# Two more pairs of hidden tiles with seven products, unscaled token blocks, and weight sums made in DRAM

## The chip, the cores and the metric

One Trainium2 core runs the whole kernel. The metric is device time in microseconds (us) of one execution; the profile adds one execution seen from inside.

## The reference

One decoder layer on 512 tokens of width 1024, in float32:

```python
x = x + 0.5 * rms_norm(swiglu(rms_norm(x, g1), w1_in, w1_out), g1_post)      # first half
h = rms_norm(x, g2); q, k, v, u = split(h @ w_mix_in)
x = x + rms_norm(concat(attention(q, k, v), s5(u)) @ w_mix_out, g2_post)     # mixing
x = x + 0.5 * rms_norm(swiglu(rms_norm(x, g3), w2_in, w2_out), g3_post)      # second half
# swiglu(h) = (silu(h @ gate) * (h @ up)) @ w_out, gate and up 1024 x 2816
# rms_norm(x, g) = x * rsqrt(mean(x*x) + 1e-6) * g
```

The change is in the second half, with preparations for it in the first half and in the boundary ahead of the second half.

## The kernel before

**Arithmetic.** Each float32 operand `t` of a product is split into a high part (`hi`, a cast on ACT) and the rest (`lo = t - hi`, a subtraction on DVE or POOL); a product is three matmuls, high x high, high x low, low x high (`mm3`). The helper `wsplit` splits weights, `split` splits activations.

**Hidden tiles.** The hidden width 2816 is 22 tiles of 128. A *plain* tile `f` takes two weight blocks (gate and up, 128 x 1024 each) against all 512 tokens: 24 matmuls a block. From tile `NSTD` on, tiles go in *pairs* with a seven-product scheme: gate and up, each halved along the 1024 inputs, are the four weight blocks a11, a12, a21, a22 (each 512 inputs for two tiles), and the tokens are halved too. A pair has seven products of 24 matmuls over 256 tokens in place of eight: in order a11, a12, c2, c1, c3, c2 + a12 and a22, with the sums c3 = a11 + a21, c2 = c3 + a22 and c1 = a21 + a22 made on DVE by `pair`. The token side of the products is four blocks as they are or subtracted (b11, b21, b22, n1) and three more sums (n2, t3, t4, in tiles `tq`). `pair` reuses the banks `wx`, `wy` and `wq` and ends with Silu, the multiplication with up, and the split into `ah`, `al`.

**Before the change** `NSTD = (8, 6)`: the first half has eight plain tiles and seven pairs, the second half six plain tiles and eight pairs. Tiles 0 and 1 of the second half are computed in `boundary`, tiles 2 to 5 in `swiglu_half` (`products`, matmuls `gu`). While they run, the token blocks are scaled by the norm's gain and by its per-token factor r (`seven`/`sums`, line 533), summed and split. The transposes of x to token-major rows for the end (`tokens_first`, matmuls `xt`) are put between these matmuls by hooks, and so are the two steps of the norm's sums (`late[0]`, `late[1]`: a matmul `st`, a small operation `nv` on DVE, a power on POOL, a matmul `rp`).

**Boundary.** `boundary` ends one part and begins the next: it adds the last output products (`yt`), and for each half of the tokens and each of eight rows of blocks `prep` forms the new x and its split on DVE and ACT, and `begin` issues 12 matmuls of the next part (`first`). POOL adds up squares.

**Output.** The hidden tiles are multiplied with the output weights in three rounds of six tiles (`outp`, matmuls `yo`) and a last one of four (`finish`, matmuls `yt`), which normalises and stores rows.

**Order.** Instructions wrapped in `fix` keep their program order on their engine; the others are placed by a scheduler that goes by program order as priority. Loads are issued from SP into `wraw` (three buffers), `wa` and `wx`; the split weights go to a ring of four (`whi`, `wlo`). DVE, ACT and POOL run ahead of PE as far as these rings allow. POOL does not issue any transfer.

Of the kernel before, what the change touches and what calls it, by code (L numbers as in the profile page):

```python
# [29 lines left out]
NSTD = (8, 6)  # L30
# [14 lines left out]
class Layer:  # L45
# [30 lines left out]


# [195 lines left out]
    def boundary(self, y, tail, ipost, half, inext, chunks):  # L273
# [40 lines left out]
        def prep(h, k, fix=lambda i: i):  # L314
# [5 lines left out]
            self.split(xh(k)[:, hs[h]], xl(k)[:, hs[h]], xk, self.g(inext, k), fix)  # L320
            self.sq_acc(acc2[:, hs[h]], xk, k == 0, nc.gpsimd)
# [46 lines left out]
        for k in range(KD):  # L368
            if k > 1:
                prep(0, k, fx if k > 5 else lambda i: i)  # L370
            begin(0, k)
            if k == 2:
                post[1][0](late, fix=fx)
            if k == 4:
                rr[1] = post[1][1]()
        for k in range(KD):
            prep(1, k)
            begin(1, k)
            if k == 3:
                pre[0][0](fixp=fx)  # L380
            if k == 6:
                pre[0][1]()
        self.xh, self.xl = xh, xl
# [6 lines left out]
    def ffn(self, n, first, scope):  # L390
# [42 lines left out]
        def outp(i, ms=range(KD), tails=None, hold=0):  # L433
# [3 lines left out]
            def part(m, k0, k1):  # L437
# [15 lines left out]
                else:  # L453
                    nc.vector.tensor_tensor(out=y(m), in0=b[m], in1=y(m), op=ALU.add)
# [20 lines left out]
        prep = sums(True)  # L475
# [5 lines left out]
        for m in range(2, KD):  # L481
# [3 lines left out]
            outp(0, (m,))  # L485
        for f in range(NSTD[0], NF, 2):
            pair(f, f in (NSTD[0], 14))
# [23 lines left out]
    def seven(self, fin, w_in, ig, r, ah, al):  # L511
# [13 lines left out]
        def sums(early=False):  # L525
# [13 lines left out]
            more[0] = (yield) or fin  # L539
            if early:  # L540
                self.pad(more[0], 192)
# [4 lines left out]
            bh, bl = [self.b16(n, F32R) for n in ("bh", "bl")] if early else (None, None)  # L546
            v = lambda t, i: t.rearrange("p (q k) c -> p q (k c)", q=4)[:, i]

            def plain(*ts):
                for t in ts:  # L550
                    i = len(blocks)
                    blocks.append((v(bh, i), v(bl, i)))
                    self.split(*blocks[i], t)

            if early:
                plain(b11)
            V.scalar_tensor_tensor(out=n2, in0=n1, scalar=-1.0, in1=b22, op0=ALU.mult, op1=ALU.subtract)
            if early:
                plain(b21)
# [6 lines left out]
            if early:  # L566
                plain(b22, n1)
# [4 lines left out]
            if not early:  # L572
                yield
                bh, bl = [self.b16(n, F32R) for n in ("bh", "bl")]
                plain(b11, b21, b22, n1)
            yield

        def block(f, up, kh):
            if up:
                t = wx() if kh else more[0].tile([P, 1024], F32, name="wa", tag="wa")  # L580
# [3 lines left out]
            nc.sync.dma_start(out=t.rearrange("p (f c) -> p f c", f=2), in_=src)  # L584
            return t
# [922 lines left out]
```

## Time and profile before

| | |
|---|---|
| median of 3 runs | 916.98 us (916.5 to 918.2) |
| the profiled execution | 916.19 us, span 914.2 us |
| busy in the span | PE 898.9, DVE 656.0, ACT 442.0, POOL 217.5 us |
| first half, mixing, second half begin at about | 0, 386, 585 us |
| plain tiles 2 to 5 of the second half | 584.72 to 634.36 us |
| moved by transfers | 106.81 MB, 117 GB/s mean |

A row of a stage gives its length, then busy time and number of instructions by engine; PE is TensorE's matmuls, PEld its weight loads, which overlap them. A row of a group gives line, engine, operation, out<-in, shapes and count, then busy time and mean duration (ns), then idle time before it and what ended that.

### The profile page before, as it was taken

To read this page: it belongs to the slowest core of one execution; us is meant where nothing else is said; L and a number is where in the kernel's file an instruction comes from. 1 tells how busy PE (TensorE), PEld (TensorE's weight loads), DVE (VectorE), ACT (ScalarE), POOL (GpSimd) and SP (SyncE) were. 2 spreads that over 40 slices of the span, in tenths; PEclk is the share of its full clock that TensorE was granted. 3 is DMA by queue.
4 is the path that set the end of the run, shared out by engine and by line. 5 is a ranking of instruction groups with operands and counts; after the bars stand their busy time and mean duration, and the time that the engine had idled before them with its cause. 6 is when DMAs were issued, how large, how long until landed. Compare 5 with 4: busy or idle time off the path is not lost.

```text
span 914.2 us, 15367 instructions
## 1 busy us (share of the span) xinstructions
PE 898.9 (98%) x6169; PEld 801.4 (88%) x6169; DVE 656.0 (72%) x1071; ACT 442.0 (48%) x685; POOL 217.5 (24%) x127
## 2 busy tenths in 40 slices
PE   9999999999999999999999999999999999999996
PEld 7787789998999989978777889888899989998995
DVE  6999786755678666758898567898368557855756
ACT  6263763553355543525745654573355514541542
POOL 0423301322123134500000025523222222221321
PEclk9999999999999999999999999999999999999999
DMA  8223662334231262283321452145222422332222
GB/s 277 94 70 115 196 248 76 107 102 137 77 119 61 68 194 86 92 221 109 116 70 51 153 167 71 29 179 180 97 93 99 133 92 93 116 116 92 92 93 92
DMA packets 47734, 106.81 MB, mean 117 GB/s; under 512 B 7824, under 2 KB 11152, under 8 KB 47120
## 3 DMA queue, kind: packets, MB, share of 16 engines
q1 hardware_dynamic: 46080, 102.21, 34.5%
q10 hardware_dynamic: 1584, 3.63, 1.1%
q8 instruction: 48, 0.79, 0.3%
q14 instruction: 22, 0.18, 0.1%
HBM read 96.13 MB, written 9.70 MB: 116 GB/s over the span
## 4 chain that ended last, share of the span: by engine, by line
PE 79%; DVE 6%; issue 2%; DMA 2%; ACT 1%; POOLq 0%; POOL 0%; DVEq 0%; SPq 0%; ACTq 0%
PE yo L144 21%; PE wx L144 18%; PE wq L144 9%; PE yt L144 6%; PE wy L144 4%; PE gu L144 4%; PE prj L144 4%; PE first L144 3%; PE prv L144 2%; PE mo L144 2%; PE ys L144 1%; PE st L144 1%; DMA w1d<-w1s 1%; PE pt L1098 1%; PE sc L144 1%
## 5 line engine op out<-in xcount | busy, mean ns | idle before, releaser
L117 ACT CAST whi<-wraw 128x1024 fp32r<-128x1024 f32 (+5 forms) x128 | 124.0, 976 | 160.3 <-PE yo L144 65.5
L119 POOL TENSOR_TENSOR wlo<-wraw,whi 128x1024 fp32r<-128x1024 f32 (+1 forms) x41 | 109.2, 2666 | 297.6 <-ACT whi L117 290.3
L119 DVE TENSOR_TENSOR wlo<-wraw,whi 128x1024 fp32r<-128x1024 f32 (+5 forms) x87 | 107.4, 1242 | 75.7 <-ACT whi L117 75.6
L144 PE MATMUL wx<-tq,whi 128*128 128x256 f32 x720 | 124.7, 276 | 0.0
L144 PEld LDWEIGHTS wx<-tq,whi 128*128 128x128 f32 x720 | 108.3, 188 | 0.0
L119 DVE TENSOR_TENSOR wlo<-wsum,whi 128x1024 fp32r<-128x1024 f32 x60 | 73.6, 1227 | 46.5 <-ACT whi L117 46.4
L117 ACT CAST whi<-wsum 128x1024 fp32r<-128x1024 f32 x60 | 63.0, 1050 | 81.8 <-PE yo L144 28.1
L144 PE MATMUL wx<-tq,wlo 128*128 128x256 f32 x360 | 99.4, 276 | 0.0
L119 POOL TENSOR_TENSOR wlo<-wx,whi 128x1024 fp32r<-128x1024 f32 x15 | 41.5, 2764 | 176.3 <-ACT whi L117 128.5
L144 PEld LDWEIGHTS wx<-tq,wlo 128*128 128x128 f32 x360 | 67.6, 188 | 0.0
L144 PE MATMUL gu<-xh,whi 128*128 128x512 f32 x168 | 67.2, 400 | 0.0
L144 PE MATMUL gu<-xh,wlo 128*128 128x512 f32 x168 | 65.7, 391 | 1.1 <-POOL wlo L119 1.1
L144 PE MATMUL wq<-bh,whi 128*128 128x256 f32 x240 | 66.2, 276 | 0.0
L144 PE MATMUL wq<-bl,whi 128*128 128x256 f32 x240 | 66.2, 276 | 0.0
L144 PE MATMUL wq<-bh,wlo 128*128 128x256 f32 x240 | 66.2, 276 | 0.0
L144 PE MATMUL gu<-xl,whi 128*128 128x512 f32 x168 | 65.5, 390 | 0.0
L144 PE MATMUL yo<-ah,whi 128*128 128x512 f32 x144 | 56.3, 391 | 0.0
L144 PE MATMUL yo<-al,whi 128*128 128x512 f32 x144 | 56.1, 389 | 0.0
L144 PE MATMUL yo<-wlo,ah 128*128 128x512 f32 x144 | 56.0, 389 | 0.0
L144 PE MATMUL yo<-whi,ah 128*128 128x512 f32 x144 | 56.0, 389 | 0.0
L144 PE MATMUL yo<-ah,wlo 128*128 128x512 f32 x144 | 56.0, 389 | 0.0
L144 PE MATMUL yo<-whi,al 128*128 128x512 f32 x144 | 56.0, 389 | 0.0
(267 smaller groups left out, 2385.0 us busy)
## 6 DMA issues: line engine op xcount, KB each, us to landing
wraw<-w1i SPq DMA_DIRECT2D x28, 512.0 KB, 3.7
wraw<-w2i SPq DMA_DIRECT2D x28, 512.0 KB, 3.6
wraw<-w2o SPq DMA_DIRECT2D x18, 512.0 KB, 3.7
wraw<-wmi SPq DMA_DIRECT2D x12, 512.0 KB, 4.1
wraw<-w1o SPq DMA_DIRECT2D x8, 512.0 KB, 4.2
wa<-w2i SPq DMA_DIRECT2D x8, 512.0 KB, 3.7
wx<-w2i SPq DMA_DIRECT2D x8, 512.0 KB, 4.0
wa<-w1i SPq DMA_DIRECT2D x7, 512.0 KB, 3.6
```

Source lines behind the costliest of these rows:

```text
L117: fix(self.nc.scalar.copy(out=hi, in_=raw))
L119: fix(eng.tensor_tensor(out=lo, in0=raw, in1=hi.bitcast(F32), op=ALU.subtract))
L144: i = self.nc.tensor.matmul(*a, **k)
L1098: self.fix(nc.tensor.transpose(b[i][:, o:o + P], sc[:, c:c + P], self.ident))
```

## The change

1. `NSTD = (8, 2)`: in the second half tiles 2 to 5 become pairs 2 and 4, ten pairs in all.
2. The pairs of the second half take token blocks that are not scaled by r: three of the four plain blocks are views of `xh`, `xl` themselves. The gate sum is multiplied by r in `pair` (DVE), up is not; r comes back per row in `finish` as `r4`. In `hidden` one multiplication goes.
3. The boundary keeps an unrounded copy of the gained x (`wide`, ACT, one per `prep`) and makes two token sums from it in eight steps (`wide_sums`, DVE). The others are made between the products of pair 2 (`begun`, `further`, `last`).
4. For every pair c3 and c1, and for the pairs 2 and 4 also c2 and c2 + a12, are made in DRAM: a copy issued from SP and an accumulating transfer issued from POOL, 512 KB each. They are spread over the first half and its boundary: each call of `more` counts one, and each 1.6 counts issue one transfer. `pair` then loads the sums (`whole`).
5. The first two weight blocks of pair 2 are loaded and split in the boundary (`self.first`), into a tile of their own.
6. Hooks between the products of pairs 2 and 4 take over the transposes and the norm's steps.

```diff
-NSTD = (8, 6)
+NSTD = (8, 2)
+EARLY = (2, 4)
+PACE = 1.6
...
+    def block_sums(self):
...
+        copy = lambda o, i: self.dma(out=o, in_=i)
+        plus = lambda o, i: self.fix(nc.gpsimd.dma_start(out=o, in_=i, accum_op=ALU.add))
+        t = lambda f, c: self.csum[f, c]
+        stages = (lambda f: copy(t(f, 3), src(f, 0, 0)), lambda f: copy(t(f, 1), src(f, 1, 0)),
+                  lambda f: plus(t(f, 3), src(f, 1, 0)), lambda f: plus(t(f, 1), src(f, 1, 1)),
+                  lambda f: copy(t(f, 2), t(f, 3)), lambda f: plus(t(f, 2), src(f, 1, 1)),
+                  lambda f: copy(t(f, 4), t(f, 2)), lambda f: plus(t(f, 4), src(f, 0, 1)))
+        for n in range(len(fs) + 1):
+            todo = []
+            if n:
+                todo += [(2, fs[n - 1]), (3, fs[n - 1])]
+            if n < len(fs):
+                todo += [(0, fs[n]), (1, fs[n])]
+            if n > 2:
+                todo.append((4 + (n - 3) // 2, EARLY[(n - 3) % 2]))
...
@@ boundary
             self.split(xh(k)[:, hs[h]], xl(k)[:, hs[h]], xk, self.g(inext, k), fix)
+            if wide:
+                fix(nc.scalar.activation(out=t, in_=xk, func=AF.Copy, scale=self.g(inext, k)))
...
             begin(0, k)
+            self.more()
...
+        if wide:
+            wide = wide(y)
         for k in range(KD):
             prep(1, k)
             begin(1, k)
+            if wide and k:
+                wide(k - 1)
...
@@ ffn
                 products(f)
+                self.more(2 + (f > 2))
...
@@ pair
-            a21, a22 = block(f, 1, 0), block(f, 1, 1)
-            c3 = wsum()
-            add(a11, a21, c3)
-            c2 = wsum()
-            add(c3, a22, c2)
-            times(X, cut(c2), n2, False)
+            then(1)
+            if four:
+                c2 = whole(f, 2)
+            else:
+                if made:
+                    c3, a22 = whole(f, 3), block(f, 1, 1)
+                else:
...
+            times(X, cut(c2), tq[0], False, 2 in lead)
...
+            if made:
+                V.tensor_tensor(out=gt, in0=gt, in1=r.unsqueeze(1).to_broadcast([P, 2, S]), op=ALU.mult)
             nc.scalar.activation(out=gt, in_=gt, func=AF.Silu)
...
+    def wide_sums(self, gx):
...
+        for kh in range(2):
+            raw = self.wp.tile([P, 1024], F32, name="wraw", tag="wraw", bufs=3)
+            self.nc.sync.dma_start(out=raw.rearrange("p (f c) -> p f c", f=2), in_=src(kh))
+            hi, lo = (room[:, kh, i] for i in range(2))
+            self.wsplit(raw, hi, lo)
...
+            if k < 4:
+                V.tensor_tensor(out=h(k, 0), in0=h(k, 0), in1=h(k, 1), op=ALU.subtract)
+            else:
+                V.scalar_tensor_tensor(out=self.n2[:, (k - 4) * HT:(k - 3) * HT], in0=h(k - 4, 0), scalar=-1.0, in1=h(k, 1),
+                                       op0=ALU.mult, op1=ALU.subtract)
...
@@ swiglu_half
+        each = {i: step for i in range(6)}
+        pair(2, (2,), hooks={**each, 0: begun, 1: further, 2: late[1], 3: last}, ahead=self.first)
+        hidden(0)
+        hidden(1)
...
+        pair(4, hooks=each)
+        step(9)
...
-        for f in range(NSTD[1], NF, 2):
-            pair(f, f in (NSTD[1], 12, 18), f == NF - 2)
+        for f in range(6, NF, 2):
+            pair(f, (0,) if f in (6, 12, 18) else (), f == NF - 2)
...
@@ finish
-            fx(V.tensor_tensor(out=yg[b, i], in0=at(y, b, i), in1=self.gt[d][:, sl], op=ALU.mult))
+            fx(V.scalar_tensor_tensor(out=yg[b, i], in0=at(y, b, i), scalar=r4[:, b:b + 1], in1=self.gt[d][:, sl],
+                                      op0=ALU.mult, op1=ALU.mult))
```

In the first half `more` is called by `ffn` after its plain tiles and output products and by `pair` between its products.

More of the change, by code (lines that the diff above doesn't have):

```diff
@@ L565, in sums @@
             yield
-            if early:
-                plain(b22, n1)
+            plain(b22, n1)
             yield
@@ L571, in sums, with pairs @@
             self.split(*tq[2], t4)
[L572 to L575, printed above, removed]
             yield
+        room = lambda: more[0].tile([P, 1024], F32, name="wa", tag="wa")
+        return sums, self.pairs(w_in, blocks, tq, wsum, gp, (room, wx), r, ah, al)
+    def pairs(self, w_in, blocks, tq, wsum, gp, rooms, r, ah, al, csum=None):
+        nc, V = self.nc, self.nc.vector
+        wa, wx = rooms
         def block(f, up, kh):
-            if up:
-                t = wx() if kh else more[0].tile([P, 1024], F32, name="wa", tag="wa")
+            if up and (kh or not csum):
+                t = wx() if kh else wa()
             else:
@@ L605, in keep, with pair @@
             return t
-        def pair(f, lead=False, late=False):
-            (b11, b21, b22, n1), (n2, t3, t4) = blocks, tq
+        def pair(f, lead=(), late=False, hooks={}, ahead=None):
             add = lambda x, z, t: V.tensor_tensor(out=t, in0=x, in1=z, op=ALU.add)
@@ L611, in pair @@
             half = lambda t, h: t[:, :, h * HT:(h + 1) * HT]
+            then = lambda i: hooks[i]() if i in hooks else None if csum else self.more()
+            made = bool(csum)
+            four = made and (f, 2) in csum
             gt = p2(gp())
             X = self.bank("wx")
-            a11 = block(f, 0, 0)
-            times(X, cut(a11), b11, True, lead)
+            if not ahead:
+                a11 = block(f, 0, 0)
+                h11 = cut(a11)
+            else:
+                h11, h12 = ahead
@@ L616, in pair @@
+            times(X, h11, blocks[0], True, 0 in lead)
             s1 = keep(X)
-            a12 = block(f, 0, 1)
-            h12 = cut(a12, True)
+            if not ahead:
+                a12 = block(f, 0, 1)
+                h12 = cut(a12, True)
+            then(0)
             Y = self.bank("wy")
-            times(Y, h12, b21, True)
+            times(Y, h12, blocks[1], True)
             V.tensor_tensor(out=half(gt, 0), in0=p2(Y), in1=p2(s1), op=ALU.add)
-            a21, a22 = block(f, 1, 0), block(f, 1, 1)
@@ L639, in pair @@
             nc.scalar.activation(out=gt, in_=gt, func=AF.Silu)
-            times(X, cut(a22, True), t4, False)
+            then(5)
+            times(X, cut(a22, not ahead), tq[2], False)
             s = f % RING
@@ L699, in outp, with begun, further, last @@
                         V.tensor_tensor(out=y(b, d), in0=b4[b], in1=y(b, d), op=ALU.add)
[L701 to L716 removed]
+        tq[0] = put(0, n2)
+        pair = self.pairs(w_in, blocks, tq, lambda: fin.tile([P, 1024], F32, name="wsum", tag="wsum", bufs=3),
+                          lambda: fin.tile([P, 1024], F32, name="gp", tag="gp"), (None, lambda: fin.tile([P, 1024], F32, name="wx", tag="wx", bufs=2)), r, ah, al, self.csum)
+        def begun():
+            blocks[3] = put(3, part(gx, 0, 0))
+            step()
+        def further():
+            third()
+            late[0]()
+        def last():
+            fourth()
+            step()
+        each = {i: step for i in range(6)}
+        pair(2, (2,), hooks={**each, 0: begun, 1: further, 2: late[1], 3: last}, ahead=self.first)
+        hidden(0)
+        hidden(1)
         self.gt = [self.acct() for _ in range(2)]
@@ L1430, in run, with more @@
         first = self.start(chunks, ipre)
+        back = self.block_sums()
+        owed = [0]
+        def more(n=1):
+            owed[0] += n
+            while owed[0] >= PACE:
+                owed[0] -= PACE
+                next(back, None)
+        self.more = more
         for p, q in zip(parts, parts[1:] + " "):
```

150 lines of the change are left out of this document (92 added, 58 removed).

## The prediction

> **What bounds the kernel now.** I read the page first (busy times, queues, chain), then the busy time by stage around the second half, then what TensorE waited for, then single stretches of DVE, ACT and POOL where the change puts work.
>
> ```profile
> span 914.2 us, 15367 instructions
> PE 898.9 (98%) x6169; PEld 801.4 (88%) x6169; DVE 656.0 (72%) x1071; ACT 442.0 (48%) x685; POOL 217.5 (24%) x127
> q1 hardware_dynamic: 46080, 102.21, 34.5%
> PE 79%; DVE 6%; issue 2%; DMA 2%; ACT 1%; POOLq 0%; POOL 0%; DVEq 0%; SPq 0%; ACTq 0%
> ```
>
> TensorE is busy for 898.9 of 914.2 us and carries 79% of the chain; all its idle time is 15.3 us. A change can win much only by taking matmuls away, and can lose wherever it makes one wait. The second half by stage (us, then busy time and count of PE, PEld, DVE, ACT, POOL, the clock, the DMA share, GB/s):
>
> ```profile
> 584.72:634.36 49.64, 48.44 (x234) 40.00 (x233) 46.22 (x54) 27.84 (x38) 19.01 (x7) 1.00 0.46 159
> 607.16:612.60 5.44, 5.44 (x25) 4.50 (x24) 5.44 (x9) 5.44 (x10) 0.00 (x0) 1.00 0.13 50
> 667.00:686.19 19.19, 19.19 (x170) 19.18 (x169) 11.93 (x12) 10.36 (x13) 4.79 (x2) 1.00 0.33 108
> 686.19:705.23 19.04, 19.04 (x170) 19.04 (x169) 15.44 (x16) 10.72 (x12) 5.92 (x2) 1.00 0.31 111
> ...
> PE xt L505 <- DVE nv L205: 1.2, 1, 1.2
> ...
> L117 ACT CAST whi<-wraw 128x1024 fp32r<-128x1024 f32 x7 | 7.4, 1053 | 8.7 <-PE wq L144 5.2 <-PE wx L144 3.6
> ```
>
> The first row is the stage that the change rewrites: tiles 2 to 5 with plain matmuls, the transposes of x between them. The second is one plain 128x1024 weight block against 512 tokens (24 matmuls): 5.44 us. The third and fourth are the first two pairs, seven products each: 19.04 us, that is 2.72 for a product, and 0.15 more where the lead splits one matmul in two. The fifth is the only wait of PE in that stage that the trace names, 1.2 us. The last, from the first three pairs, is the cast that splits a loaded block: 1.05 us, and the idle time before it ends when PE frees room (`wq`, `wx`), not when a load lands.
>
> **The change part by part.**
>
> *Products.* Tiles 2 to 5 are 8 plain blocks, 8 x 5.44 = 43.52 us. Two pairs are 14 products, 14 x 2.72 = 38.08 us. Gain 5.44, less 0.15 for the lead split that pair 2 gets in addition. The eight groups of transposes and the sums of the norm (49.64 - 43.52 - 1.2 = 4.9 us) keep their number and only move, so they cost the same. The wait of 1.2 hangs on the old order (the sums' result stands in DVE's queue behind the scaling of x); that queue goes, so I take it out and price the new waits on their own. Most that can be won: 5.44 - 0.15 + 1.20 = 6.49 us.
>
> *Work removed from DVE.* Sixteen scalings, sums and splits of the x blocks leave this stage; two weight sums per pair go from pair 6 on (1.22 us each, below), and one 1.22 us product with r per pair comes. PE does not wait in the pair stage now, and the cover (DVE 15.44 of 19.04 us) gets better, so this is worth nothing.
>
> *The boundary before the second half.* ACT gets 16 scaled copies of x, DVE eight subtractions of 128x256, and two weight blocks are split there where one was.
>
> ```profile
> 551.26:584.72 33.46, 32.92 (x280) 32.24 (x280) 27.74 (x57) 16.84 (x39) 16.96 (x20) 1.00 0.15 49
> L319 DVE TENSOR_TENSOR x<-ymix,x 128x256 f32<-128x256 f32 x16 | 10.0, 639 | 0.1
> L317 DVE SCALAR_TENSOR_TENSOR ymix<-ymix,sm,rp 128x256 f32<-128x256 f32 x16 | 7.2, 470 | 0.0
> L302 DVE TENSOR_TENSOR ymix<-yt,ymix 128x256 f32<-128x256 f32 x2 | 0.8, 414 | 0.0
> L119 DVE TENSOR_TENSOR tq<-wraw,tq 128x1024 fp32r<-128x1024 f32 x1 | 1.2, 1212 | 0.0
> L176 ACT ACTIVATE sq<-x 128x256 f32<-128x256 f32 x14 | 5.6, 403 | 0.8 <-POOL acc L178 0.8
> 580.84 0.48 DVE L167 SCALAR_TENSOR_TENSOR xl<-x,sm,xh 128x256 fp32r<-128x256 f32 x1 [0.58 <-ACT xh L166]
> 583.27 0.37 PE L144 MATMUL first<-xh,whi 128*128 128x256 f32 x1
> ```
>
> DVE is busy 27.74 of 33.46 us here. Seven of the eight steps stand ahead of the last block: 4 x 0.41 + 3 x 0.47 = 3.05 us, and the second weight split adds 1.21: 4.26 us. DVE's last result is ready at 580.84 + 0.48 = 581.32 and PE takes it at 583.27, 1.95 us later; DVE also idled 0.58 us before it. So 4.26 - 1.95 - 0.58 = 1.7 us reach PE. ACT's 16 copies at the 0.40 of a square (6.4 us) and one more cast (1.05) fit its 33.46 - 16.84 = 16.6 us of idle time. Bounds: 0, if the scheduler finds other gaps (DVE has 5.7 us of them), to 4.3 with no slack used. I take 1.7.
>
> *Pairs 2 and 4.* Pair 2 starts on the token blocks as they are and on weights already split, so its first two products (5.44 us) wait for nothing. By the end of those the split of n2 and of the loaded sum c2 must be done, two times a cast of 1.05 and a subtraction of 1.21 on two engines in turn: some 3.5 us, inside 5.44. Later products need one such split per 2.72 us, besides the third and fourth token sums (1.22 each, and their splits). In 19 us DVE has about 10 operations of 1.2 and three of 0.69, 14 us: it fits, with little air, and the norm's sums now have only one product (2.72 us) between their two PE steps. Bounds 0 (all inside) to 2.5 (twice the old wait); I take 0.6, half the old one, since DVE's queue here is shorter than before.
>
> *The sums in DRAM.* Ten pairs times two copies and two accumulating transfers, and two of each more for the two early pairs: 24 copies on SP's queue and 24 accumulates on POOL's, 512 KB each, one for every 1.6 calls, all issued before the attention part begins. All loads together hold 16 engines for 34.5% of 914.2 = 315 us for 102.21 MB, so 512 KB cost 1.62 us of all engines. By stage, before:
>
> ```profile
> 60.00:145.00 85.00, 83.03 (x436) 67.48 (x435) 68.54 (x99) 47.94 (x80) 20.84 (x9) 1.00 0.52 170
> 145.00:340.00 195.00, 195.00 (x1458) 184.70 (x1457) 129.34 (x131) 92.80 (x107) 47.96 (x20) 1.00 0.32 103
> ...
> PE gu L144 <- POOL wlo L119: 1.1, 1, 1.1
> 178.78 3.51 POOL L119 TENSOR_TENSOR wlo<-wx,whi 128x1024 fp32r<-128x1024 f32 x1 [11.26 <-ACT whi L117]
> 185.66 0.39 PE L144 MATMUL wx<-tq,whi 128*128 128x256 f32 x2
> 368.00 0.71 POOL L207 TENSOR_TENSOR p<-nv,mhalf 128x2 f32<-128x2 f32 x1 [2.37 <-DVE nv L205]
> 170.84 0.34 SPq L123 DMA_DIRECT2D wraw<-w1o  x1
> wraw<-w2i SPq DMA_DIRECT2D x28, 512.0 KB, 3.6
> ```
>
> Some 14 steps fall into the first stage: 14 x 1.62 = 23 us, a share of 0.52 + 0.27 = 0.79; 30 into the second, 0.32 + 0.25 = 0.57. If an accumulate cost double, 0.90 and 0.70. Both stay under 1, and in the pairs the casts wait for PE and not for loads, so bandwidth costs little. POOL is the open point: no row of this kernel shows a transfer issued from POOL. An accumulate also waits there for its copy, with POOL's splits behind it. In the pair stage a POOL split ends at 178.78 + 3.51 = 182.29 and PE needs it at 185.66: 3.4 us of slack. The plain stage has none once: PE waited 1.1 us for such a split. Bounds for one hold: nothing, to the 3.6 us of a landing, if POOL is held as long as the transfer takes. The nearest row for a small job of POOL is the 0.71 us power; at about that hold, 3.4 us hide it in the pairs, and I take 0.5 us for all of the first half (bounds 0 and 8, worked out in rival C). SP issues 24 more transfers at 0.34 us each, 8 us over some 350, and none of the copies waits but four in the early pairs' chains, whose inputs were issued two rounds before.
>
> *The end.* The product with r stands in the last pair between the sum and the Silu:
>
> ```profile
> 882.69 0.69 DVE L638 TENSOR_TENSOR gp<-wq,kp 128x512 f32<-128x512 f32 x1 [1.96 <-PE wq L144]
> 883.41 1.06 ACT L639 ACTIVATE gp<-gp 128x1024 f32<-128x1024 f32 x1 [2.50 <-DVE gp L638]
> 885.24 0.62 ACT L163 CAST ah<-gp 128x512 fp32r<-128x512 f32 x1 [0.76 <-DVE gp L644]
> 886.02 1.46 DVE L164 TENSOR_TENSOR al<-gp,ah 128x512 fp32r<-128x512 f32 x2
> 886.60 0.39 PE L144 MATMUL yt<-whi,ah 128*128 128x512 f32 x1
> 887.05 0.39 PE L144 MATMUL yt<-whi,al 128*128 128x512 f32 x1
> L609 DVE TENSOR_TENSOR wsum<-wsum,wraw 128x1024 f32<-128x1024 f32 x2 | 2.4, 1220 | 0.0
> ```
>
> The low part of the first half is ready at 886.02 + 0.73 = 886.75, PE takes it at 887.05. A product of 128x1024 at 1.22 us ahead of the Silu moves it to 887.97: PE waits 0.9 us. Bounds 0.5 (the high part's own delay: 885.86 + 1.22 against 886.60) to 1.2. In the other pairs the next product covers it. The three-operand form in the final gains adds at most 0.1 on the last one.
>
> *Sum.* -6.49 + 1.7 + 0.6 + 0.5 + 0.9 + 0.1 = -2.7 us. The profiled execution took 916.19 us (span 914.2 and 2 around it), 0.8 under the median 916.98: 916.19 - 2.7 = 913.5.
>
> **The rivals.**
>
> A, more of it stays: the boundary's additions find gaps, no new waits, POOL unnoticed. -6.49 + 0.9 + 0.1 = -5.5: 910.7. For it: DVE's 5.7 us of idle time in the boundary; against: four of its waits there are for ACT, which gets more work.
>
> B, the boundary takes it all back. The 0.64 us mean of the additions to x, beside the 0.41 of an addition of the same size from PSUM, shows that operations with both inputs in SBUF run slow while POOL sums squares (POOL 16.96 of 33.46 us). The new steps are of that kind: 7 x 0.64 + 1.21 - 2.53 = 3.2 us, and with DVE late into pair 2, 2.0 us of waits there: -6.49 + 3.2 + 2.0 + 0.5 + 1.0 = +0.2: 916.4.
> The Trainium skill (SBUF — State Buffer, "Who interferes with whom") says that a DVE instruction with two SBUF inputs contends with a GpSimd instruction that reads SBUF. By that rule B's price is the one to use for the new steps; the trace's 639 ns against 414 ns agree with it.
>
> C, slower: POOL is held by its accumulates. Four of them are issued in the first boundary, while POOL owes the power at 368.00 on which the second half's scale hangs. Held 3.6 us each, two ahead of it less its 2.4 us of idle time delay it by 4.8 us; twenty more exceed the 3.4 us slack of a split by 0.2 to 0.3 each where they meet one, say 3 us. 913.5 + 4.8 + 3 - 0.5 = 920.8. It ends slower from a hold of about 3.5 us on; the 3.6 of a landing speaks for it, the short POOL rows and the idle POOL (24%) against.
> The Trainium skill (DMA: Bandwidth & Descriptors, "SWDGE vs HWDGE vs iDMA") says that accumulating transfers can only come from GpSimd, whose software builds the descriptors. By that rule POOL's time is really spent, as in C; no run so far shows how much.
>
> **How the numbers follow.** The sum as worked out 0.47 (own range 911.5 to 915.5), A 0.20, B 0.18, C 0.15. The range reaches from a little under A to between B and C: 909.8 to 919.5, which leaves out some 0.15. A measurement here tells about 0.2%, 1.8 us, from no change: under 915.1 is faster (A, nearly all of the sum's case: 0.65), up to 918.8 the same (most of B and the rest of the sum: 0.19), above slower (C and a little of B: 0.16).
>
> **What would show it.** Right, if the stage after the boundary takes 43 to 44 us instead of 49.64 with no `gu` rows, every later pair still takes 19.04, the last `first` row of the boundary comes 1 to 2 us later, and `yt` waits near 1 us for `al` in the last pair. B shows as waits of `first` on DVE; C as POOL's `wlo` or the power standing late behind its queue, and gaps of PE ahead of 400 us. A DMA share near 1 in the 60 to 145 us stage would make it wrong in a way that I give no own case.

## The result, and the profile after

The changed kernel takes 924.79 us (median of 5 runs, 921.53 to 927.32) against 917.43 (5 runs, 916.5 to 918.2): 1.008 times as long, 95% interval 1.0054 to 1.0106. The forecast was 913.5. The profiled execution took 924.79 us, span 923.0, 8.8 us more span than before.

The page of the changed kernel: busy times, the transfer queues (packets, MB, share of 16 engines), and three groups of transfers (count, size, median us to landing).

```profile
span 923.0 us, 15765 instructions
PE 898.5 (97%) x6314; PEld 807.5 (87%) x6314; DVE 637.0 (69%) x1054; ACT 454.4 (49%) x706; POOL 231.2 (25%) x149
q1 hardware_dynamic: 53408, 122.14, 40.7%
q0 software_dynamic: 6528, 12.58, 8.3%
...
wraw<-w1i SPq DMA_DIRECT2D x28, 512.0 KB, 5.7
c<-w2i POOLq DMA_DIRECT2D x24, 512.0 KB, 8.7
c<-w2i SPq DMA_DIRECT2D x20, 512.0 KB, 6.7
```

TensorE's idle time grew from 15.3 to 24.5 us, and its busy time fell by 0.4 instead of the 5.3 that fewer matmuls promised: about 3 us of the difference (an estimate) are matmuls that ran at half the clock, as shown below. The accumulating transfers have a queue of their own, q0: 8.3% of 923.0 us of all engines for 12.58 MB is 6.1 us per MB, twice the 3.1 of the plain queue q1.

Where the 8.8 us are is seen by the distance between the first matmuls of each stage (us). `w1t`, `kb` and `kc` are matmuls that prepare weights of the s5 part; `kc` transposes what ACT copies to `kt`. They stand between matmuls of the first half. `prj` is the first product of the mixing. The columns e1 to e8 are the experiments further down.

| stage | before | after | e1 | e2 | e3 | e4 | e5 | e8 |
|---|---|---|---|---|---|---|---|---|
| start to `w1t`, in the plain tiles | 74.30 | 78.07 | 74.09 | 75.78 | 74.12 | 74.31 | 74.73 | 74.15 |
| first `yo` to `kc` | 4.93 | 6.82 | 5.18 | 6.26 | 8.53 | 5.32 | 5.55 | 7.32 |
| `kc` to the first pair | 41.36 | 42.59 | 41.35 | 41.34 | 42.63 | 41.31 | 41.34 | 43.94 |
| seven pairs and their `yo` rounds | 188.02 | 188.02 | 188.0 | 188.0 | 188.0 | 188.0 | 188.02 | 188.03 |
| boundary into mixing, from `first` | 24.93 | 26.04 | 24.93 | 25.61 | 24.93 | 29.86 | 24.93 | 26.52 |
| mixing | 148.78 | 149.43 | 150.99 | 148.89 | 148.5 | 148.5 | 150.15 | 149.56 |
| boundary into the second half | 26.24 | 28.12 | 29.39 | 28.13 | 29.35 | 29.37 | 28.13 | 29.38 |
| tiles 2 to 5 | 49.64 | 45.46 | 44.35 | 45.48 | 44.21 | 44.36 | 45.33 | 44.20 |
| later pairs | 218.21 | 218.50 | 219.21 | 218.24 | 218.44 | 218.42 | 218.51 | 218.28 |
| last `yt` products | 22.10 | 23.07 | 22.97 | 23.08 | 23.09 | 23.09 | 23.07 | 23.07 |

Mixing begins at 393.98 us instead of 385.98: 8.0 us are lost in the first half, whose arithmetic did not change. The second half and its boundary lose 1.9, win 4.2, and lose 0.3, 1.0 and, behind the last matmul (7.53 against 6.89 us), 0.6. The mixing's 0.65 is within what it scatters by in the other columns. Of the stages left out of the table one moved by more than 0.1 us, the last mixing products ahead of the boundary (23.72 to 24.25). The first row scatters, too: in the experiments without a DRAM sum among the plain tiles it lies between 73.0 (e12) and 75.1 us (e14).

Windows of the changed kernel (length, then busy time and count of PE, PEld, DVE, ACT, POOL, the clock, the DMA share, GB/s):

```profile
40.00:60.00 20.00, 16.75 (x72) 13.53 (x71) 19.98 (x74) 5.62 (x8) 8.26 (x4) 0.98 0.42 80
60.00:75.00 15.00, 15.00 (x62) 12.22 (x61) 15.00 (x35) 9.25 (x19) 7.25 (x2) 0.91 0.33 105
104.00:157.00 53.00, 50.30 (x272) 40.83 (x271) 36.59 (x39) 30.30 (x47) 12.50 (x8) 0.97 0.97 303
157.00:345.00 188.00, 188.00 (x1419) 178.60 (x1419) 126.45 (x129) 90.52 (x104) 59.69 (x32) 1.00 0.64 174
595.78:641.24 45.46, 43.82 (x380) 43.53 (x378) 34.96 (x36) 30.84 (x42) 9.52 (x6) 1.00 0.65 204
```

The kernel before in two of these stretches:

```profile
40.00:60.00 20.00, 20.00 (x90) 16.57 (x89) 19.98 (x60) 7.23 (x13) 4.51 (x2) 1.00 0.22 74
104.00:150.00 46.00, 45.19 (x229) 36.84 (x228) 32.43 (x35) 26.56 (x42) 6.00 (x3) 1.00 0.59 202
```

PE falls from 20.00 to 16.75 busy at 40 to 60 us, and the mean clock is 0.91 behind it. Narrower windows of the changed kernel show what that mean is made of:

```profile
57.70:59.10 1.40, 1.40 (x6) 1.18 (x7) 1.40 (x3) 0.00 (x1) 1.40 (x1) 1.00 0.00 0
59.17:62.55 3.38, 3.38 (x9) 2.63 (x8) 3.38 (x8) 0.00 (x0) 1.53 (x1) 0.50 0.27 33
62.60:75.00 12.40, 12.40 (x56) 10.24 (x55) 12.40 (x28) 9.25 (x19) 6.54 (x1) 1.00 0.32 118
```

The clock is at half for 3.4 us, which costs some 1.7 us of matmul time, and full before and after. The 0.97 from 104 us on is a second such stretch, at 113.8 us. From 104 us on the DMA share is 0.97 where it was 0.59. The pairs after that carry a share of 0.64 at no loss. What PE waited for in the changed kernel (us in total, times, longest):

```profile
PE gu L174 <- DVE wlo L149: 3.2, 1, 3.2
PE kc L1148 <- ACT kt L1144: 2.7, 1, 2.7
PE first L174 <- DVE xl L197: 2.2, 6, 0.8
PE rp L174 <- POOL r L237: 1.4, 1, 1.4
```

The first wait is a weight split that DVE makes late, and DVE is late because of POOL. POOL near 38 us, before and then after:

```profile
38.11 3.56 POOL L972 MEMSET gb<- 128x2048 f32 x2
```

```profile
37.96 2.31 POOL L90 DMA_DIRECT2D c<-w2i  x2
39.28 4.56 POOL L1097 MEMSET gb<- 128x2048 f32 x2
```

DVE in the same stretch, before and then after:

```profile
39.26 2.44 DVE L944 COPY pw<-pp 128x16 f32<-128x16 f32 x1
51.35 1.22 DVE L119 TENSOR_TENSOR wlo<-wraw,whi 128x1024 fp32r<-128x1024 f32 x1
```

```profile
38.81 5.06 DVE L1024 TENSOR_SCALAR pp<-pp 128x16 f32<-128x16 f32 x1
56.43 1.22 DVE L149 TENSOR_TENSOR wlo<-wraw,whi 128x1024 fp32r<-128x1024 f32 x1
```

And PE after:

```profile
57.70 0.50 PE L174 MATMUL gu<-xh,wlo 128*128 128x512 f32 x1 [3.25 <-DVE wlo L149]
```

Accumulating transfers issued by POOL (over 1 us each) stand ahead of two zero fills. A DVE operation on 16 columns, 0.17 us elsewhere in the trace, takes 5.06 us and ends at 43.87, when POOL's fills end (39.28 + 4.56 = 43.84). Before, the same coupling cost DVE 2.44 us. The split that PE needs comes at 56.43 instead of 51.35, and PE stands for 3.25 us. Of these 5.1 us, 2.2 are the later end of DVE's hold (43.87 against 41.70); the rest is other work that DVE now has ahead of the split.
The Trainium skill (SBUF — State Buffer, "Who interferes with whom") says that DVE, in its two-port modes, and GpSimd lock one shared port pair for a whole instruction, and that the other blocks; DVE's end at POOL's end agrees with it, though DVE was held over two fills here, and the trace does not show in which mode it ran.

### The profile page after: what moved, and what is told of

The parts are those of the page before. It is cut to its first block, busy times and chain, and to the rows that moved or that the text cites. A ratio compares the mean times of both kernels' runs of the same rounds, so it can differ in the third digit from the quotient of the medians.

```text
span 923.0 us, 15765 instructions
## 1 busy us (share of the span) xinstructions
PE 898.5 (97%) x6314; PEld 807.5 (87%) x6314; DVE 637.0 (69%) x1054; ACT 454.4 (49%) x706; POOL 231.2 (25%) x149
## 3 DMA queue, kind: packets, MB, share of 16 engines
q0 software_dynamic: 6528, 12.58, 8.3%
## 5 line engine op out<-in xcount | busy, mean ns | idle before, releaser
L149 POOL TENSOR_TENSOR wlo<-wraw,whi 128x1024 fp32r<-128x1024 f32 (+1 forms) x38 | 97.4, 2563 | 290.3 <-ACT whi L147 275.3
L174 PE MATMUL wx<-tq,whi 128*128 128x256 f32 (+1 forms) x817 | 142.1, 277 | 0.4 <-ACT kp L656 0.3
L174 PEld LDWEIGHTS wx<-tq,whi 128*128 128x128 f32 x817 | 123.0, 188 | 0.7 <-ACT kp L656 0.7
L147 ACT CAST whi<-wsum 128x1024 fp32r<-128x1024 f32 x68 | 71.2, 1048 | 84.8 <-PE yo L174 28.1
L174 PE MATMUL wx<-tq,wlo 128*128 128x256 f32 x408 | 112.7, 276 | 0.0
L174 PE MATMUL gu<-xh,wlo 128*128 128x512 f32 x112 | 44.6, 398 | 3.2 <-DVE wlo L149 3.2
L174 PE MATMUL gu<-xh,whi 128*128 128x512 f32 x112 | 45.4, 406 | 0.0
L174 PE MATMUL first<-xl,whi 128*128 128x256 f32 (+1 forms) x144 | 42.9, 298 | 2.3 <-DVE xl L197 2.2
L174 PE MATMUL gu<-xl,whi 128*128 128x512 f32 x112 | 44.1, 394 | 0.0
L174 PE MATMUL first<-xh,whi 128*128 128x256 f32 (+1 forms) x144 | 42.7, 297 | 0.8 <-ACT xh L196 0.8
L174 PE MATMUL first<-xh,wlo 128*128 128x256 f32 (+1 forms) x144 | 41.8, 291 | 0.0
```

The source lines that it names most:

```text
L147: fix(self.nc.scalar.copy(out=hi, in_=raw))
L149: fix(eng.tensor_tensor(out=lo, in0=raw, in1=hi.bitcast(F32), op=ALU.subtract))
L174: i = self.nc.tensor.matmul(*a, **k)
```

## The experiments

Each was timed beside the kernel before; ratios are to that kernel, with a 95% interval. e1 to e4 ran in one session, e5 to e8, e9 to e11 and e12 to e15 in three more.

**What in the first half costs: e1 to e4.** My theory: issue from POOL. The rival: the traffic.

```diff
 # e1_no_sums: whole() loads a plain block of the weights, nothing is issued in DRAM
-            nc.sync.dma_start(out=t, in_=csum[f, c].rearrange("p f c -> p (f c)"))
+            nc.sync.dma_start(out=t.rearrange("p (f c) -> p f c", f=2),
+                              in_=w_in[f:f + 2, :, :S].rearrange("f p c -> p f c"))
-        back = self.block_sums()
+        back = iter(())
```

> The changed kernel without its 48 transfers in DRAM: where a sum is loaded, a plain weight block of the same size is loaded, so the sums are left out and every later load stays. Theory T (the transfers cost the first half its 8.0 us, by traffic or by holding POOL): the attention part starts again at about 386 us instead of 394 us, and the time is 924.8 - 8.0 = about 917. Rival R (the first half is slow because the scheduler placed other instructions anew): it keeps 4 us or more of the 8, 921 or above. Both leave the second half as it is: boundary about 2.4 us longer than before, plain stage 4.2 us shorter, end 1.6 us longer.

916.87 us, ratio 0.9999 (0.9987 to 1.0011). Mixing begins as before: the whole loss of the first half hangs on the transfers. The second half alone wins nothing.

```diff
 # e2_tiny: as e1, and all 48 transfers at their places, of 16 partitions (64 KB)
+        copy = lambda o, i: self.dma(out=o[:16], in_=i[:16])
+        plus = lambda o, i: self.fix(nc.gpsimd.dma_start(out=o[:16], in_=i[:16], accum_op=ALU.add))
```

> As the kernel without sums, but with the 24 copies and 24 accumulates issued at their places, each on 16 of 128 partitions (64 KB): the issue on SP and POOL stays, seven eighths of the traffic goes. Theory P (POOL's issue of an accumulate, 1.04 to 1.57 us, pushes POOL's fills and holds DVE): the wait of 3.2 us near 57 us stays, the attention part starts at 390 to 392 us, time 921 to 923. Theory D (traffic on the 16 DMA engines): like the kernel without sums, 917.

920.46 us, 1.0029 (1.0017 to 1.0041). Issue with an eighth of the bytes costs 1.5 us in the plain tiles, 1.3 at `kc` and 0.7 in the boundary into mixing.

```diff
 # e3_sp_copies: all 48 as plain 512 KB copies from SP; what was accumulated goes to unread tiles
-        plus = lambda o, i: self.fix(nc.gpsimd.dma_start(out=o, in_=i, accum_op=ALU.add))
+        def plus(o, i):
+            spare.append(self.dr.tile([P, 2, S], F32, name=f"d{len(spare)}"))
+            self.dma(out=spare[-1], in_=i)
```

> All 48 transfers are plain copies from SP, the 24 accumulates into DRAM tiles that nobody reads (so the sums are wrong by what is not added); POOL issues nothing. Theory P: the wait near 57 us goes, 4 us or more come back, 919 to 921. Theory D: the copies cost half of an accumulate on the engines (48 x 1.62 = 78 us against 115 us), so between a third and a half of the loss goes in the 104 to 157 us stage only, 922 to 923.

922.95 us, 1.0062 (1.004 to 1.0084), its profiled execution 919.59. Without POOL the plain tiles (74.12) and the boundary (24.93) lose nothing, but `kc` comes 3.6 us late and the stage behind it loses 1.3. So both theories hold: in the plain tiles and the boundary it is POOL's issue, while `kc` loses 1.3 us in e2 and 3.6 in e3. Windows of e2, then of e3:

```profile
40.00:60.00 20.00, 18.14 (x73) 14.57 (x72) 19.98 (x80) 5.62 (x8) 6.66 (x2) 0.92 0.04 7
104.00:155.00 51.00, 48.86 (x252) 40.24 (x253) 36.14 (x38) 29.88 (x46) 10.74 (x8) 1.00 0.65 215
```

```profile
104.00:155.00 51.00, 46.58 (x230) 38.05 (x229) 34.04 (x37) 28.31 (x45) 6.45 (x4) 0.97 0.91 314
```

In e2 the DMA share at 40 to 60 us is 0.04 and PE still loses time there; in e3 POOL issues no transfer and the stretch at a share of 0.91 loses time. In the changed kernel ACT's copy to `kt` waits 1.12 us for the transfer `w1d<-w1s` of the s5 weights; in e3 DVE waits 2.83 us for such a transfer, and ACT's queue, with `kt` in it, for DVE. Whether the bytes make these transfers late, or the copies that stand between them in SP's queue, is not separated: e3 has both. The loss behind `kc` (1.23 and 1.3 us) is about what the half clock costs there.

```diff
 # e4_late: the whole change, transfers from the first pair on
-                self.more(2 + (f > 2))
...
-            self.more()      # between the first output products
...
-PACE = 1.6
+PACE = 1.15
```

> The full change, with its transfers beginning only with the first pair: the calls after the plain tiles and the first output round are left out and one transfer goes out per 1.15 calls in place of 1.6. If what matters is that they meet the state-space parameters between 35 and 157 us, as both P and D say, 6.9 us of the 8.0 come back: 918, with the pairs of the first half still at 19.04 us each. If the pairs can't carry them (48 transfers, 115 us of engine time in some 215 us with a share of 0.32 already there: 0.85), products wait and the time stays at 922 or above.

919.88 us, 1.0025 (1.0014 to 1.0037). Everything up to the boundary is as before; the boundary, with five accumulates in it, takes 29.86 instead of 24.93. PE in it:

```profile
378.89 0.48 PE L174 MATMUL first<-xl,whi 128*128 128x256 f32 x1 [1.93 <-DVE xl L197]
```

The split on DVE for which it waits, beside an accumulate that POOL issues from 376.72 on for 1.07 us, took four times the 0.47 of the splits a little later:

```profile
376.96 1.88 DVE L197 SCALAR_TENSOR_TENSOR xl<-x,sm,xh 128x256 fp32r<-128x256 f32 x1
```

**e5_pairs: all transfers in the pairs.**

```diff
 # as e4, and
             begin(0, k)
-            self.more()
...
-PACE = 1.6
+PACE = 1.0
```

> The whole change, but all 48 transfers in DRAM are handed out in the seven pairs of the first half and the second product with its output weights, one at each place; none in the plain tiles, the first output product or the boundary. Theory (the sums cost only where they are issued: POOL's issue holds DVE in the plain tiles and in the boundary, the traffic holds loads between the plain tiles and the pairs; the pairs have room): the first projection of the mixing stage starts at 385.5 to 387, as before (385.98, against 393.98), the seven pairs stay at 188.0, the time is 916.5 to 918.5. Rival (the transfers cost much the same wherever they run): the pairs grow by 3 to 6 us, the time is 920 to 924.

916.4 us, 0.9986 (0.9975 to 0.9997). The boundary is back at 24.93, and the pairs hide everything, at a DMA share of 0.84 (before 0.32, at 145 to 340 us):

```profile
150.00:338.00 188.00, 188.00 (x1419) 178.60 (x1419) 127.07 (x128) 89.56 (x103) 68.36 (x41) 1.00 0.84 219
```

Mixing begins at 387.01 us, 1.0 later than before (0.6 at `kc`, 0.4 in the plain tiles, which scatter by more). The rival, a cost wherever they run, is out: place matters, not amount.

**e8_memset: the zero fills ahead of the accumulates.**

```diff
 # the changed kernel, in ssm_params
+        gb = [pool.tile([P, NP, T, 2, 16], F32, name="gb", tag="b8") for _ in range(2)]
+        for q in range(2):
+            self.fix(nc.gpsimd.memset(gb[q], 0.0))
         cnt = [0]
```

> The changed kernel as it is, but the two zero fills of 128x2048 on POOL, which stand behind three accumulates at 39 us, come at the head of the parameter work, ahead of every accumulate. Theory (the accumulates push the fills back, DVE's small operations wait for the fills, and the late weight split makes PE wait 3.25 us and lowers its clock): the plain tiles go from 78.07 to 74.2 to 75.2, the time from 924.8 to 921 to 922. Rival (the hold is the issue of the accumulates itself, on POOL's splits and on DVE's small operations all along): 77 to 78 for the plain tiles, 924 to 925.

The plain tiles take 74.15 us: all 3.9 us come back, the theory of the fills holds. The whole did not follow: 924.98 us, 1.0077 (1.006 to 1.0093). The next stages lose 1.9 us more than in the changed kernel (`kc` and the stage behind it, 51.26 against 49.41), with the heavy traffic still there and the clock at 0.50 from 109.8 to 116.6 us; the profiled execution is 2.4 us shorter (922.42), and where the other executions lost that, no trace shows.

```profile
40.00:60.00 20.00, 20.00 (x90) 16.57 (x89) 20.00 (x86) 7.53 (x11) 6.79 (x3) 1.00 0.56 128
60.00:75.00 15.00, 15.00 (x70) 12.39 (x69) 15.00 (x31) 10.29 (x21) 9.88 (x4) 1.00 0.36 115
104.00:155.00 51.00, 47.80 (x229) 38.84 (x228) 33.99 (x37) 28.32 (x44) 10.56 (x8) 0.93 0.98 297
```

**The end: e6, e11 and e9.**

```diff
 # e6_end: on e5
             V.tensor_tensor(out=half(gt, 0), in0=p2(Y), in1=p2(s1), op=ALU.add)
+            by_r = lambda h: V.tensor_tensor(out=half(gt, h), in0=half(gt, h), op=ALU.mult, in1=...)   # r, half h
+            if made and not four:
+                by_r(0)
...
-                V.tensor_tensor(out=gt, in0=gt, in1=r..., op=ALU.mult)
+                by_r(1)
...
-        (Square with scale=r4, gain product with scalar=r4, constant 4.0 * EPS)
+        (both without r4; constant e4 = 4.0 * EPS / r4 ** 2 per row)
+        e4 = self.sp.tile([P, 4], F32, name="e4", tag="e4")
```

> As the kernel with all transfers in the pairs, and the end lightened: the gate of the first half of tokens is multiplied by r right behind its sum, so that only the other half (0.69 us) stands ahead of Silu; r4 is taken into the constant of the last norm, so that Square and the product with the gain carry no scale. Theory (the product with r and the scales are what the end lost): the stage from the first of the last products to PE's end goes from 23.1 to 22.2 to 22.4, the tail behind it from 7.5 to 6.9 to 7.1, together 1.2 to 1.6 us below the kernel without it. Rival (the wait of the last products is the split of the last block's hidden values, which stays): PE's stage stays at 23.0, and 0.3 to 0.6 us is gained.

926.81 us, 1.0089 (1.007 to 1.0107): both theories miss. The end did get shorter (22.44 for the last products), but the pairs of both halves grew, 188.0 to 191.4 and 218.5 to 223.3 us, though no line of the first half's pairs was touched. What did change for them is where in SBUF they lie: `e4` took a small buffer of its own ahead of later pools.

```diff
 # e11_shift: e5 and one unused tile
         self.sp = pool("sp", 2)
+        self.sp.tile([P, 4], F32, name="shift", tag="shift")
 # e9_end: e6 with e4 in a buffer that exists
-        e4 = self.sp.tile([P, 4], F32, name="e4", tag="e4")
+        e4 = self.sp.tile([P, 4], F32, name="e4", tag="p4")
```

> As the kernel with all transfers in the pairs, with one thing added: an unused tile of 16 bytes with two buffers, ahead of all pools made later, and nothing else. Theory (addresses in SBUF set the matmul time in the pairs): pairs of 191 and 223 us, matmuls of 256 columns 283 ns, the whole 923 to 926. Rival (what slowed the pairs was in the edit of the end): pairs 188.0 and 218.5, the whole 916 to 917.

> The lightened end again (gate's first half times r early; no scales in the last Squares and gain products), but the new 16-byte column sits in a buffer that exists already, so that no tile behind it moves in SBUF; in the run before, the column had a buffer of its own, and the pairs of both halves, the first half's untouched by the edit, grew from 188.0 to 191.4 and from 218.5 to 223.3 us (matmuls of 256 columns 283 ns instead of 277). Theory (the shift of all later tiles by 32 bytes did that, the end itself is better): pairs back at 188.0 and 218.2 to 218.8, the last products 22.4, the whole 914.8 to 915.8. Rival (the reordered products in the pairs slow the matmuls): the second half's pairs stay at 222 or more.

e11: 926.37 us, 1.0096 (1.0081 to 1.0111), pairs 191.37 and 223.17. e9: 916.33 us, 0.9986 (0.9976 to 0.9997), pairs 188.02 and 218.39. The largest matmul group (count, busy time, mean ns), in e5 and in e11:

```profile
L174 PE MATMUL wx<-tq,whi 128*128 128x256 f32 x815 | 141.9, 277 | 0.4 <-ACT kp L653 0.3
```

```profile
L175 PE MATMUL wx<-tq,whi 128*128 128x256 f32 x815 | 148.7, 283 | 0.3 <-ACT kp L654 0.3
```

A shift of two 16-byte buffers costs the kernel 10 us: 277 becomes 283 ns in the matmuls that read the token sums `tq`, and some that read `tw` grow as much. Matmuls of the same size that read `xh` hardly change, in e5 and in e11:

```profile
L174 PE MATMUL wy<-xh,whi 128*128 128x256 f32 x72 | 20.0, 277 | 0.0
L175 PE MATMUL wy<-xh,whi 128*128 128x256 f32 x72 | 20.0, 277 | 0.0
```

Why the place of some tiles does that, no run shows. In e9 the last products take 22.56 us (23.07 without the edit), and 7.22 us follow them (7.53): 0.8 us won where 1.2 to 1.6 was expected, and 2.0 lost in tiles 2 to 5, which grew from 45.33 to 47.36. There PE and POOL read:

```profile
599.21 0.71 PE L174 MATMUL rp<-ident,r 128*128 128x128 f32 x4 [1.89 <-POOL r L237]
```

```profile
600.00:612.00 12.00, 12.00 (x94) 12.00 (x93) 4.57 (x7) 5.33 (x8) 2.40 (x1) 0.86 0.58 194
```

A wait of 1.89 us for the norm's factor `r`, and a mean clock of 0.86 behind it: 0.50 from 600.8 to 604.1 us, 1.7 us more.

**The token steps behind the boundary: e7 and e10.**

```diff
 # e7_steps: on e6; e10_steps: on e9, with the moved operations, split and prep(1, k) in fix,
 # and the spread of the first half's norm in the first pair
-            if wide and k:
-                wide(k - 1)
...
         def begun():
+            for k in range(KD):
+                self.wide(k)
+            tq[0] = put(0, n2)
```

> As the kernel with the lightened end, and the eight DVE steps of the token sums with the split of n2 moved out of the boundary into the first pair, behind its first product. Theory (DVE, busy 35 of 36.9 us, bounds the boundary): from its first product to the stage behind it 29.4 becomes 25 to 27, the stage behind it stays within 0.7 us of 44.3, and 2 to 4 us is gained: 911.5 to 914. Rival (ACT's copies and the two early weight splits lengthen the boundary, or the first pair then waits for its token sums): boundary and stage together stay at 73 to 74, no gain.

> As the kernel with the lightened end, and the eight token steps and the split of n2 held in program order behind the boundary's last split of tokens, and the spread of the first half's norm on PE moved from the boundary into the first pair. In the run before, the scheduler drew the steps into the boundary again, and POOL's power of 128x2 took 7.10 us among DVE's back-to-back operations, with PE waiting 4.7 us for it. Theory (DVE bounds the boundary): the boundary from its first product to the stage behind it is 25.5 to 27, the stage 44.3 to 45.3, the whole 912 to 914. Rival (DVE's work is only moved, the first pair waits for n2's split): boundary and stage together 72.5 to 74, the whole 915 to 916.

e7: 928.93 us, 1.0113 (1.0098 to 1.0128), boundary 33.12. It carries the shift of e6, too, so only its stage is read. e10: 925.42 us, 1.0094 (1.0071 to 1.0117), boundary 33.07, tiles 2 to 5 51.91. Both theories missed in both. In e7 the scheduler drew the steps back into the boundary. POOL there, and DVE:

```profile
586.28 7.10 POOL L237 TENSOR_TENSOR r<-nv,mhalf 128x2 f32<-128x2 f32 x1 [3.29 <-DVE nv L235]
```

```profile
586.86 1.42 DVE L755 SCALAR_TENSOR_TENSOR n<-ymix 128x256 f32<-128x256 f32 x4
...
591.61 1.21 DVE L792 SCALAR_TENSOR_TENSOR ymix<-n,ymix 128x1024 f32<-128x1024 f32 x1
596.20 1.38 DVE L149 TENSOR_TENSOR wlo<-wsum,whi 128x1024 fp32r<-128x1024 f32 x1 [3.38 <-ACT whi L147]
```

POOL's power on two columns takes 7.10 us instead of the 0.71 that stands in the profile before: it ends at 593.38, half a microsecond after DVE's back-to-back row of operations (591.61 + 1.21 = 592.82), and PE waited 4.7 us for it. In e10 the same power, in the first pair, took 5.63 us (from 602.20) and cost PE 5.2; besides, the fixed order made PE wait 3.4 us for ACT's `xh` in the boundary. That DVE's row holds POOL is not shown: in the changed kernel this power, at 591.01, took 1.16 us beside DVE operations that follow each other as closely.

**The later norm: e12 and e13.**

```diff
 # e12_hooks: on e9
-        pair(2, (2,), hooks={**each, 0: begun, 1: further, 2: late[1], 3: last}, ahead=self.first)
+        pair(2, (2,), hooks={**each, 0: begun, 1: third, 2: late[0], 3: last, 4: late[1]}, ahead=self.first)
```

> As the kernel with the lightened end, but in the first pair of the second half the norm's sums go to the place behind the third product and its spread behind the fifth, so that POOL's power of 128x2 has two products' time more before PE asks for it. In the run without this, PE waited 1.89 us for that power at 597 us and its clock was 0.86 from 600 to 612. Theory (the wait and the slower clock behind it are what the stage after the boundary lost): no wait of PE for r in that stage, the stage from the boundary to the third output product 47.36 -> 44.0 to 44.6, the whole 912.5 to 914. Rival (the stage is long because its DVE work is late, whatever PE asks for): 46 to 47.4, the whole 915.5 to 916.5.

913.59 us, 0.997 (0.9958 to 0.9982): faster by 0.3% than the kernel before, and faster than the changed kernel. Of the 2.5 us between the spans of the two profiled executions, 1.3 stand in the plain tiles (72.99 us), which the edits do not touch. Tiles 2 to 5, first to last, in e12:

```profile
586.49:630.77 44.28, 43.67 (x379) 43.47 (x378) 37.09 (x42) 31.35 (x42) 10.01 (x6) 1.00 0.64 206
599.00:611.00 12.00, 12.00 (x107) 12.00 (x106) 7.96 (x14) 8.63 (x12) 3.10 (x2) 1.00 0.73 235
```

47.36 became 44.28, with no wait for r and no lower clock: PE asks later for what DVE and POOL still make late (the power begins at 599.10).

How much of that is the wait is better seen with the boundary ahead of it. The same second half took 28.1 and then 45.3 to 45.5 us in the changed kernel and e5, but 29.4 and 44.2 to 44.4 in e3, e4 and e8, where PE waited 1.3 us for `xl` at the boundary's end and 0.8 instead of 1.4 for `r`. Together that is 73.5 to 73.7 us in all five (75.9 before); e9 takes 75.5 and e12 72.4.

```diff
 # e13_light: on e12, the steps of e7 and the spread in the first pair, not fixed
```

> As the kernel with the later norm, and the eight token steps and n2's split behind the boundary, not held in order, with the spread of the first half's norm moved into the first pair too (as in the run where the fixed order made PE wait for ACT, but without that order). Theory (DVE's order bounds the boundary): boundary from its first product to the stage behind it 24 to 26.5 against 28.1, the stage 44 to 45, the whole 909.5 to 912. Rival (the steps are drawn in again and the first pair waits): boundary and stage together not under 72, the whole 913 to 915.

917.57 us, 0.9997 (0.9985 to 1.0009). The boundary gets 1.7 us shorter (26.48), but tiles 2 to 5 take 49.84: PE waits 3.2 us for ACT's `kp` in the first pair, and the clock is at 0.50 from 592.9 to 599.6 us. The wait that the rival named came, with a loss above its 913 to 915: the work is moved, not hidden.

**What the boundary pays for: e14 and e15**, both on e5.

```diff
 # e14_no_tokens: prep without the scaled copy, step() returns at once (token sums left out)
-            if wide:
-                fix(nc.scalar.activation(out=t, in_=xk, func=AF.Copy, scale=self.g(inext, k)))
 # e15_no_ahead: no early load and split
-        self.first = []
-        for kh in range(2):
+        self.first = None
+        for kh in ():
```

> As the kernel with all transfers in the pairs, without ACT's 16 scaled copies of the tokens and without the eight token steps: the token sums of the second half are left out (their buffers hold other values). Prices them: if the prediction's boundary term holds (seven steps of DVE on the path), the boundary is 25.5 to 27 us; if DVE isn't the bound, 28 as with them.

> As the kernel with all transfers in the pairs, but the first pair's two weight blocks are loaded and split in the pair itself, as in the other pairs, not ahead of the boundary's second half. Prices the early split: by the prediction's term (1.21 us of DVE on the path for the second one) the boundary is 1.0 to 2.4 us shorter than 28.1; what the first pair then waits for its first blocks shows in the stage behind (0 to 3 us more).

e14: 916.41 us, 0.9988 (0.9977 to 1.0); its boundary takes 30.36, not less, as one wait of PE for `xl` of 1.61 us and 3.4 us at half the clock (1.7 us; 0.94 over the stage) fall into it. Taking both off leaves 27.0, which is an estimate and no clean price; boundary and stage together take 73.7 us, as with the tokens (73.5 in e5). e15: 922.71 us, 1.006 (1.0042 to 1.0078). PE in the first pair of e15:

```profile
588.73 0.58 PE L174 MATMUL wx<-xh,whi 128*128 128x256 f32 x1 [3.31 <-ACT whi L147]
593.67 0.58 PE L174 MATMUL wx<-xh,wlo 128*128 128x256 f32 x1 [4.14 <-DVE wlo L149]
```

The first of these waits lies in the 29.93 us up to the stage's first matmul; without it the boundary is 26.6, 1.5 us less than with the early splits. The early splits cost the boundary that and save the pair 7.5 us of waits, and the clock was at 0.50 for 10.2 us from the end of the first wait on.

## Why the prediction was wrong

By the profiled executions the change was to win 2.7 us and lost 8.8. Of the 11.5 us between, 7.5 are in the sums in DRAM, 1.9 in the second half's boundary and the stage behind it, 0.6 at the end, and 1.5 are small drifts of other stages.

*The sums in DRAM: the step that failed.* +0.5 us was taken for the first half, with bounds 0 and 8, and 8.0 was measured, the upper end. POOL's issue of an accumulate costs 1.1 us (26.1 us for the 24 in the changed kernel), not much more than the 0.71 assumed. But the step looked for the harm on POOL's own splits, and it fell on DVE, through fills that POOL ran later (3.8 us, e8), and on the additions of the boundary into mixing (1.1 us; e4 makes it 4.9, e5 nothing). And "bandwidth costs little" was right for the pairs, where even a share of 0.84 is free, and wrong ahead of them: a share of 0.97 stood in the stretch from 104 us (forecast 0.90 at the most for 60 to 145; its own terms give 0.92), and 3.1 us were lost there, by a longer wait for `kt` (2.70 us, before 0.81) and the half clock that came with it. The text had named a share near 1 as an own way to be wrong and given it no case.

*Products and waits.* -6.49 + 0.6 = -5.9 was forecast; tiles 2 to 5 went from 49.64 to 45.46, -4.2. The stage without `gu` rows is there, but forecast at 43 to 44. The largest missing part is one wait, 1.4 us for `r`. POOL's power took its 0.71 us there; what came late is DVE's `nv` ahead of it. PE's sum `st` was done at 602.0 us, and `nv` stood behind sums and splits that follow each other on DVE. DVE and then PE in the changed kernel:

```profile
604.17 1.21 DVE L149 TENSOR_TENSOR wlo<-wsum,whi 128x1024 fp32r<-128x1024 f32 x1
605.31 0.68 DVE L681 TENSOR_TENSOR gp<-wy,kp 128x512 f32<-128x512 f32 x1
605.91 0.14 DVE L235 TENSOR_SCALAR nv<-st 128x2 f32<-128x2 f32 x1
```

```profile
606.89 0.71 PE L174 MATMUL rp<-ident,r 128*128 128x128 f32 x4 [1.39 <-POOL r L237]
```

So the old wait of 1.2 was taken out because a queue on DVE goes, and the new order has such a queue with other work in it; that DVE's queue is shorter than before was the wrong step here. The term for waits was 2.3 (6.49 less 4.18) in place of 0.6; e12, where PE asks later, takes 1.1 us less than the changed kernel for boundary and stage together.

*The boundary.* +1.7 was forecast, +1.9 measured, which is partly luck: in e3, e4 and e8, with the same second half, it was +3.1, and the stage behind it 1.2 us shorter than in the changed kernel. Only the two together can be held against the forecast: -2.3 us measured, -4.2 forecast. e15 gives about 1.5 of it to the early splits (1.21 was taken for one), while e14 gave no clean price for the token steps. That slack absorbed the rest, as worked out, is not shown.

*The end.* +0.9 and +0.1: PE's stage lost 0.97, as forecast (0.57 ahead of the first product with `ah`, the rest in the three steps behind it), but 0.64 more went behind PE's last matmul, where every gain product and Square carries a scale. In the changed kernel, DVE and then PE:

```profile
890.61 1.23 DVE L718 TENSOR_TENSOR gp<-gp,rs 128x1024 f32<-128x1024 f32 x1
```

```profile
894.36 0.50 PE L174 MATMUL yt<-whi,ah 128*128 128x512 f32 x1 [0.41 <-ACT ah L193]
```

The product of 1.23 us was priced at 1.22 and stands where it was placed; e9 won 0.5 of the 0.97 and 0.3 of the 0.64 back.

*The rivals.* B, the boundary, is out at this size: boundary and stage together still win 2.3 us. But what the boundary and the new waits took back, 4.2 us (6.49 less 2.3), lies between the 2.3 of the sum and the 5.2 of B, and B's price for a new step was near (683 and 544 ns on average, 0.64 us assumed). C's end on the slower side came, but not its mechanism: POOL was held 1 to 1.6 us by an accumulate, not 3.6, no split of POOL's made PE wait longer, and the power in the boundary into mixing took its 0.7 us. Three accumulates, where C put four, were issued there and did harm, through DVE.

## What to carry to other kernels

Work "hidden on an idle engine" has a price that depends on which operations of other engines grow longer beside it, so ask of every place where it is issued what DVE does there and which wait of PE is nearest; stages of back-to-back matmuls with loads far ahead took 48 transfers for nothing, while stages with a tight chain paid. Place a chain of small operations on busy engines so that PE asks for its result later than seems needed: one product more between the norm's two steps on PE took away the wait here. After an edit that adds a buffer, compare the mean matmul time, operand by operand, of stages that were not edited, before the edit itself is judged.

## What the hardware showed that was not expected

- Two unused 16-byte buffers lengthened matmuls of 256 columns that read `tq` from 277 to 283 ns, but not those that read `xh`: +10 us of 916 (e11 against e5).
- A power of two columns on POOL, 0.71 us in the profile before, took 7.10, 5.63 and 11.65 us in e7, e10 and e13, while DVE was over 89% busy; beside a DVE as busy it took 1.16 us in the changed kernel, so what decides it is open. A 16-column operation of DVE took 5.06 us under POOL's fills.
- What a gap of PE costs in clock did not follow its length. Each time the clock was at 0.50 for 3.4 us (some 1.7 us of matmul time), or for two or three times as long. One such stretch came behind gaps of 1.61 (e14), 1.86 (e2), 1.89 (e9), 1.93 (e4), 3.25 (changed kernel) and 4.42 us (e3), none behind 1.80 (e6), 1.91 (e5) and 2.14 us (e2, at `kc`).
The Trainium skill (TensorE: Matmul & The Clock Gate, Part 1) has the clock drop after an idle window of about 3.4 us; here some gaps of 1.6 to 1.9 us were enough, and the measurement decides.
- An accumulating transfer in DRAM takes twice the engine time of a copy (6.1 against 3.1 us per MB) and lands in 8.7 us, a copy of the same size in 6.7 (medians of the changed kernel).
